# A 528-byte pitch for the blocks of the split activations, in a float32r encoder kernel on Trainium2

## The chip, the cores and the metric

The kernel runs on one core of one Trainium2 chip. The metric is the device time of one execution in microseconds (us), as the median of several runs. TensorE does the products, ScalarE (ACT) and VectorE (DVE) prepare their operands and read their results, GpSimd (POOL) does small work, and SyncE (SP) issues the loads of the weights.

## The reference

A trunk of two layers over 256 tokens of width 1024. Each layer is x += 1/2 SwiGLU(RMSNorm(x)), then a mixer (a gated delta rule in both directions, and a latent attention, merged by gates), then a second SwiGLU. What matters here is the number of dense products:

```python
def swiglu(x, w_gate, w_up, w_down):
    return (jax.nn.silu(x @ w_gate) * (x @ w_up)) @ w_down   # 1024 -> 2816 -> 1024, four times
h = rmsnorm(x, norm_mix[l])
... = split_cols(h @ w_in[l])                                # 1024 -> 4784, twice
x = x + (gates[:, :, 0] * y_a + gates[:, :, 1] * y_b) @ w_out[l]
```

## The kernel before

Every dense product is done in float32r, with each operand split into a high and a low half that are both exact in that type. Three passes make one product: high by high, high by low, low by high. `mm3` (lines 129 to 135) issues them, and its three matmul lines are L133, L134 and L135:

```python
for t in ts:
    a1, a2 = (v[:, t * P:(t + 1) * P] for v in a)
    T.matmul(ps[t][:, :n], lhsT=a1, rhs=w[0], start=start, stop=False)
    T.matmul(ps[t][:, :n], lhsT=a1, rhs=w[1], start=False, stop=False)
    T.matmul(ps[t][:, :n], lhsT=a2, rhs=w[0], start=False, stop=stop)
```

The stationary operand (`lhsT`, loaded into the array by a weight load of its own before each matmul) is a block of activations, 128 channels by 128 tokens, which is 512 bytes in each partition. The moving operand (`rhs`) is a strip of the weight matrix of up to 512 columns, 2048 bytes in each partition. So TensorE reads two places of SBUF in turn for each product: the 512 bytes of the next block, and the 2048 bytes of the running strip.

The activations lie in pairs of tiles. `xh` and `xl` (halves of the normed x, [128, 8 chunks, 256 tokens]) feed the gate and up products and the input projection of the mixer. `hh` and `hl` ([128, 22 chunks, 256 tokens]) feed the down products of SwiGLU. `fr2` tiles ([128, 2 chunks, 256 tokens]) feed the smaller products of the mixer. In all of them a chunk takes 1024 bytes, token tile 0 and token tile 1 of 512 bytes each, with nothing between.

One group of lines has the roles swapped. `qkv_group` (L536) loads a 128 by 128 block of the weights as stationary operand and moves all 256 tokens of a chunk of `xh` or `xl` past it.

The tiles are placed one behind the other in each partition. In the compiled program of this kernel their first bytes are, counted modulo 512: `xh` 0, `xl` 0, the three buffers each of the weight halves `whi` and `wlo` 0, `hh` and `hl` 64, `fr2` 96. For the last down product the kernel takes the weights of the last six chunks from a pool of its own (`fin`, in `finale`); those buffers start at 64 modulo 512. Strips of 512 columns start at 0 or 2048 bytes in their buffer.

The weights come from HBM in transfers of up to 1 MB on SP's queue (`raw`), ACT rounds them to the high half (L122), DVE makes the low half (L123). The activations are turned by transposes on TensorE into PSUM (`to_chan`, L183), and `split` writes the two halves: L104 and L105 for `hh` and `hl`, L107 and L108 with a gain for `xh` and `xl`. Order on each engine is chosen when the program is built, by a planner that simulates a timeline; it keeps the order of the code where priorities say so and fills gaps with what is ready.

Of the kernel before, what the change touches and what calls it, by code (L numbers as in the profile page):

```python
# [11 lines left out]
F32 = mybir.dt.float32  # L12
F32R = mybir.dt.float32r
# [7 lines left out]
P = 128  # L21
D = 1024
# [15 lines left out]
def encoder_trunk(ctx: ExitStack, tc: tile.TileContext, x, positions, norm_ffn1, ffn1_w_gate, ffn1_w_up,  # L38
# [23 lines left out]
    # the tensor engine's clock rises while the first loads run  # L62
# [8 lines left out]
    # columns of gains: ffn1 (8 per layer), mix, ffn2, q latent (3), kv latent (2), gdn (1)  # L71
# [21 lines left out]
    xh = main.tile([P, NKC, S], F32R, name="xh")  # L93
    xl = main.tile([P, NKC, S], F32R, name="xl")
# [6 lines left out]
    def split(hi, lo, ps, gain=None):  # L101
        """hi + lo = gain * ps, both exact in float32r."""
        if gain is None:
            A.copy(out=hi, in_=ps)  # L104
            V.tensor_tensor(out=lo, in0=ps, in1=hi.bitcast(F32), op=ALU.subtract)  # L105
        else:
            A.activation(out=hi, in_=ps, func=AF.Copy, scale=gain)  # L107
            V.scalar_tensor_tensor(out=lo, in0=ps, scalar=gain, in1=hi.bitcast(F32), op0=ALU.mult,  # L108
                                   op1=ALU.subtract)

    def weights(src, nk, w, pool=wpool):
        """A [nk*128, w] slice of weights, as (hi, lo) tiles of up to 1024 elements a partition."""
        raw = wpool.tile([P, 2048], F32, tag="raw", name="raw", bufs=3)
        nc.sync.dma_start(out=raw[:, :nk * w].rearrange("p (k c) -> p k c", c=w),
                          in_=src.rearrange("(k p) c -> p k c", p=P))
        per = 1024 // w
        res = []
        for k0 in range(0, nk, per):
            n = min(per, nk - k0)
            hi = pool.tile([P, 1024], F32R, tag="whi", name="whi", bufs=3)  # L120
            lo = pool.tile([P, 1024], F32R, tag="wlo", name="wlo", bufs=3)
            A.copy(out=hi[:, :n * w], in_=raw[:, k0 * w:(k0 + n) * w])  # L122
            V.tensor_tensor(out=lo[:, :n * w], in0=raw[:, k0 * w:(k0 + n) * w], in1=hi[:, :n * w].bitcast(F32),  # L123
                            op=ALU.subtract)
            for k in range(n):
                res.append((hi[:, k * w:(k + 1) * w], lo[:, k * w:(k + 1) * w]))
        return res

    def mm3(ps, a, w, n, start, stop, ts=range(NT)):
        """ps[t] (+)= a^T w in three passes, for the token tiles ts."""  # L130
        for t in ts:
            a1, a2 = (v[:, t * P:(t + 1) * P] for v in a)
            T.matmul(ps[t][:, :n], lhsT=a1, rhs=w[0], start=start, stop=False)  # L133
            T.matmul(ps[t][:, :n], lhsT=a1, rhs=w[1], start=False, stop=False)  # L134
            T.matmul(ps[t][:, :n], lhsT=a2, rhs=w[0], start=False, stop=stop)  # L135

    def dense_t(acts, src, c0, w, evac, tail=4, pool=wpool):
        """evac(t, psum [128 tokens, w]) of acts @ src[:, c0:c0+w]; acts: (hi, lo) [128, tokens] of each chunk.
        The last chunks (tail or fewer) go through for one token tile, then for the other."""
# [19 lines left out]
    def dense(ah, al, nk, src, c0, w, evac, **kw):  # L159
        dense_t([(ah[:, k, :], al[:, k, :]) for k in range(nk)], src, c0, w, evac, **kw)  # L160

    def dense_halves(acts, parts):
        """dense_t for two parts (src, c0, evac) of 512 columns: the first half of the chunks for both, then the second."""
# [11 lines left out]
    def to_chan(srcs, hi, lo, kc, gain0=None):  # L175
        """Transposes srcs[t] ([128 tokens, n*128]) into chunks kc.. of hi / lo [128, chunk, tokens]."""
        n = srcs[0].shape[1] // P
        for j in range(0, n, 2):
# [6 lines left out]
            if gain0 is None:  # L185
                split(hi[:, kc + j:kc + j + m, :], lo[:, kc + j:kc + j + m, :],
                      pt[:, :m * S].rearrange("p (c s) -> p c s", s=S))
            else:
                for i in range(m):
                    g = gain0 + j + i  # L190
                    split(hi[:, kc + j + i, :], lo[:, kc + j + i, :], pt[:, i * S:(i + 1) * S], gcol[:, g:g + 1])
# [7 lines left out]
    def x_done(t, cg):  # L199
        """Half cg of x's tile t is final: sum of squares."""  # L200
        A.activation(out=junk, in_=x_sb[:, t, cg * 512:(cg + 1) * 512], func=AF.Square,
                     accum_out=state["ss"][:, t, cg:cg + 1])
# [28 lines left out]
    def ffn(w_gate, w_up, w_down, next_gain, hook=None):  # L231
# [3 lines left out]
        with tc.tile_pool(name="ffn", bufs=1) as fp:  # L235
            hh = fp.tile([P, NFC, S], F32R, name="hh")
            hl = fp.tile([P, NFC, S], F32R, name="hl")
            for c0 in range(0, DFF, 512):
# [17 lines left out]
                else:  # L256
                    dense_halves([(xh[:, k, :], xl[:, k, :]) for k in range(NKC)],
# [12 lines left out]
    def finale(down):  # L270
        """The last x, its norm, the result; x of the first half lies by its gains before the second is there."""
# [37 lines left out]
    def mixer_consts(tmp):  # L309
# [16 lines left out]
        alog = const.tile([P, depth, 8], F32, name="alog")  # -exp(A_log)  # L326
# [12 lines left out]
        # m[p, f]  # L339
# [6 lines left out]
        # half[:, 0]: partition % 32 < 16, half[:, 1]: the others  # L346
# [7 lines left out]
        # the off-diagonal 16-blocks of the 32-blocks on the diagonal: below it (mlo) and above it (mup)  # L354
# [11 lines left out]
        # rotary tables  # L366
# [42 lines left out]
    def mixer(l, next_gain):  # L409
# [7 lines left out]
        with tc.tile_pool(name="mix", bufs=1) as mp:  # L417
# [16 lines left out]
            def rstd_row():  # L434
                """rstd along the free axis, the same in every partition."""
# [26 lines left out]
            def to_chan2(srcs, gains):  # L462
                """Chunks of 128 channels, two to a tile: a list of (hi, lo) [128, tokens]."""
                n = srcs[0].shape[1] // P
                res = []
                for j in range(0, n, 2):
# [13 lines left out]
                    res += [(hi[:, i, :], lo[:, i, :]) for i in range(m)]  # L480
# [18 lines left out]
            def gdn_scalars():  # L499
# [4 lines left out]
                # softplus(a) = max(a, 0) + log1p(exp(-|a|))  # L504
# [14 lines left out]
            qkT = mp.tile([P, 8, S], F32, name="qkT")  # L519
            vT = {}  # lies in ysb until ysb is written  # L520
# [4 lines left out]
            def qkv_group(grp):  # L525
                """Two of the twelve chunks of channels."""
# [3 lines left out]
                # one group of sums after the other: they share a bank. The second takes the weights from the last on  # L530
                for c in range(2):
                    cc = slice(c * P, (c + 1) * P)
                    terms = [m for kc, (wh, wlo) in enumerate(ws)
                             for m in ((wh, xh[:, kc, :]), (wh, xl[:, kc, :]), (wlo, xh[:, kc, :]))]
                    for i, (w, a) in enumerate(terms[::-1] if c else terms):
                        T.matmul(pc[:, c], lhsT=w[:, cc], rhs=a, start=(i == 0), stop=(i == len(terms) - 1))  # L536
# [16 lines left out]
                # 2 silu(.); the lengths and |k| v below take account of the 2  # L553
# [5 lines left out]
            def lengths(c0):  # L559
                """1/|.| of four of the eight heads of q and k, a column for each head."""  # L560
                pss = gdp()[:, :4 * NT * 32].rearrange("p (c t s) -> p c t s", c=4, t=NT)
                for c in (0, 2):
# [3 lines left out]
                    for g in range(4):  # L566
                        # the sums for the tokens of group g, in each of its partitions
# [28 lines left out]
            def mla_dense(hf):  # L596
                """q, k, v of four heads, token-major, rotary parts turned."""
# [22 lines left out]
            def mla_heads(q, k, v):  # L620
                """attend(pair of heads), of the four that q, k, v hold."""
# [15 lines left out]
                def attend(c):  # L637
# [36 lines left out]
                    oT.append((hi[:, c, :], lo[:, c, :]))  # L674
# [4 lines left out]
            LA, Z, egc, cs = {}, {}, {}, {}  # L679
            LAd = {}  # L680
            for d in range(2):
                LAd[d] = mp.tile([P, NT, NH, 2, P], F32, name=f"LA{d}")  # [.., 0, :] for q, [.., 1, :] for k
# [7 lines left out]
            def gdn_coeffs():  # L690
# [3 lines left out]
                # -beta / |k|^2  # L694
# [17 lines left out]
            def gdn_decay(t):  # L712
                """E[j, h, i]: decay from token j to token i of the tile, 0 where i comes before j."""
                for d in range(2):
# [10 lines left out]
                    if t == d:  # L725
                        # first tile of this direction: decay of each token up to the carried state
# [5 lines left out]
                    # hi_m[p, f] holds where f is at or after p in this direction  # L732
# [25 lines left out]
            def gdn_base():  # L758
                """XC, ZC: inverses (and transposes) of the 16-blocks on the diagonal, each block in a partition of its
                own meanwhile."""  # L760
# [47 lines left out]
            def inv_zero():  # L808
                """Z = X^T = (1 + L)^-T from the inverted 16-blocks: blocks of 32, 64, 128 in turn."""
# [23 lines left out]
            def inv2(d):  # L833
# [9 lines left out]
                # the 64-block that the last step takes X from  # L843
# [41 lines left out]
            def gdn_first(d):  # L885
                """First tile of direction d: its solution, and what it adds to the other tile."""
# [39 lines left out]
            def gdn_out(t):  # L926
# [10 lines left out]
                # o here is -|q| sqrt(128) times the true one, zs_t is 2 silu(z) / rstd  # L937
# [118 lines left out]
    new_norm()  # L1056
    state["squares"] = False  # of the input: once its products run
# [32 lines left out]
```

## Time and profile before

| what | value |
|---|---|
| median of 3 runs | 1267.02 us (1266.68 to 1269.48) |
| span of the profiled execution, first to last instruction | 1260.2 us |
| median less span | 6.8 us |
| TensorE busy | 98% of the span |
| mean granted TensorE clock | 0.993 |

The device time of the profiled execution itself isn't recorded beside its span; the median of the runs lies 6.8 us above the span, and that is taken as what lies around it. In the rows below PE is TensorE's matmul side and PEld its weight loads. Each matmul's duration in the rows overlaps with the next one's, so the time that a product costs is the distance from one start to the next, and not the duration.

### The profile page before, as it was taken

Reading aid. Unit: us, or ns where it says so; the run is one execution under the profiler, and the core shown is the slowest. Engines: PE = TensorE matmul, PEld = TensorE weight load, DVE = VectorE, ACT = ScalarE, POOL = GpSimd, SP = SyncE. Lnnn points to the kernel's source line nnn. Section 1 sums busy time; section 2 is a strip of 40 time slices with the busy share of each in tenths; the row PEclk is TensorE's granted clock in tenths of the full one; section 3 lists DMA queues with packets and bytes.
Section 4 is the critical chain, followed back from the end, with each engine's and each line's share of the span. In section 5 each row is a group of like instructions: output and inputs, shape, how many; then the busy total and the mean of one; then the engine's idle time right before and its main releaser. Section 6 shows DMA issues by size and latency. Waiting matters only on the chain.

```text
span 1260.2 us, 17612 instructions
## 1 busy us (share of the span) xinstructions
PE 1230.4 (98%) x7064; PEld 1031.9 (82%) x7064; DVE 774.1 (61%) x1127; ACT 623.4 (49%) x911; POOL 132.5 (11%) x237
## 2 busy tenths in 40 slices
PE   9999999899999999999999999998999999999997
PEld 6888889777988788888888888897778787888886
DVE  5655556986757665554555554588876576555554
ACT  6554445546445455443445443465555455544443
POOL 1000001445001000000000000015540000000010
PEclk9999999999999999999999999999999999999999
DMA  7554554435222555555555555543442245565552
GB/s 266 175 197 153 198 184 157 153 119 167 71 99 95 164 176 181 187 169 198 182 187 182 185 167 201 177 147 123 150 162 74 68 134 184 168 199 179 188 184 84
DMA packets 114576, 202.70 MB, mean 161 GB/s; under 512 B 4107, under 2 KB 30399, under 8 KB 114495
## 3 DMA queue, kind: packets, MB, share of 16 engines
q1 hardware_dynamic: 114031, 200.52, 47.8%
q8 instruction: 55, 0.90, 0.3%
q10 hardware_dynamic: 464, 1.06, 0.2%
q14 instruction: 26, 0.21, 0.1%
HBM read 200.52 MB, written 1.05 MB: 160 GB/s over the span
## 4 chain that ended last, share of the span: by engine, by line
PE 88%; DVE 4%; POOL 4%; issue 1%; ACT 1%; DMA 0%; POOLq 0%; SPq 0%; ACTq 0%
PE acc L133 24%; PE acc L134 23%; PE acc L135 23%; PE acc L536 4%; PE ms L183 2%; DVE wlo L123 2%; POOL bt L783 1%; PE ms L671 1%; PE ms L642 1%; POOL t L785 1%; PE gd L134 1%; PE gd L135 1%; PE gd L133 1%; PE gd L912 1%; DVE cv L551 1%
## 5 line engine op out<-in xcount | busy, mean ns | idle before, releaser
L123 DVE TENSOR_TENSOR wlo<-raw,whi 128x1024 fp32r<-128x1024 f32 (+3 forms) x388 | 471.2, 1217 | 371.0 <-ACT whi L122 369.0
L122 ACT CAST whi<-raw 128x1024 fp32r<-128x1024 f32 (+3 forms) x388 | 398.8, 1031 | 435.9 <-PE acc L135 392.0
L134 PE MATMUL acc<-wlo,xh 128*128 128x512 f32 (+3 forms) x968 | 360.7, 374 | 0.0
L135 PE MATMUL acc<-whi,xl 128*128 128x512 f32 (+3 forms) x968 | 357.5, 372 | 0.0
L133 PE MATMUL acc<-whi,xh 128*128 128x512 f32 (+3 forms) x968 | 344.9, 376 | 0.1
L134 PEld LDWEIGHTS acc<-wlo,xh 128*128 128x128 f32 x968 | 182.4, 188 | 29.8 <-issue 0.4
L133 PEld LDWEIGHTS acc<-whi,xh 128*128 128x128 f32 x968 | 181.4, 188 | 30.4 <-ACT xh L107 0.8
L135 PEld LDWEIGHTS acc<-whi,xl 128*128 128x128 f32 x968 | 182.1, 188 | 29.3
L134 PE MATMUL acc<-wlo,hh 128*128 128x512 f32 x352 | 138.9, 395 | 0.0
L135 PE MATMUL acc<-whi,hl 128*128 128x512 f32 x352 | 138.7, 394 | 0.0
L133 PE MATMUL acc<-whi,hh 128*128 128x512 f32 x352 | 129.1, 397 | 0.0
L135 PEld LDWEIGHTS acc<-whi,hl 128*128 128x128 f32 x352 | 65.9, 187 | 16.1
L133 PEld LDWEIGHTS acc<-whi,hh 128*128 128x128 f32 x352 | 65.9, 187 | 15.9
L134 PEld LDWEIGHTS acc<-wlo,hh 128*128 128x128 f32 x352 | 65.9, 187 | 15.3
L133 PE MATMUL acc<-whi,fr 128*128 128x512 f32 (+1 forms) x152 | 60.9, 407 | 9.2 <-DVE pre L543 7.9
L134 PE MATMUL acc<-wlo,fr 128*128 128x512 f32 (+1 forms) x152 | 61.0, 404 | 0.0
L135 PE MATMUL acc<-whi,fr 128*128 128x512 f32 (+1 forms) x152 | 58.2, 400 | 2.3 <-DVE fr L108 2.3
L536 PE MATMUL acc<-xl,whi 128*128 128x256 f32 x192 | 55.6, 289 | 0.0
L536 PE MATMUL acc<-xh,whi 128*128 128x256 f32 x192 | 55.5, 291 | 0.0
L536 PE MATMUL acc<-xh,wlo 128*128 128x256 f32 x192 | 53.3, 288 | 0.0
L551 DVE SCALAR_TENSOR_TENSOR cv<-pre,ccol,cv 128x256 f32<-128x256 f32 x96 | 51.6, 569 | 0.0
L246 ACT ACTIVATE sil<-acc,rstd 128x512 f32<-128x512 f32 (+1 forms) x48 | 31.0, 654 | 29.5 <-PE acc L135 29.4
(298 smaller groups left out, 1273.3 us busy)
## 6 DMA issues: line engine op xcount, KB each, us to landing
raw<-in_ffn_w_up_dram SPq DMA_DIRECT2D x40, 1024.0 KB, 4.9
raw<-in_ffn_w_down_dram SPq DMA_DIRECT2D x40, 1024.0 KB, 4.9
raw<-in_ffn_w_gate_dram SPq DMA_DIRECT2D x38, 1024.0 KB, 4.9
raw<-in_w_in_dram SPq DMA_DIRECT2D x32, 1024.0 KB, 4.8
raw<-in_w_out_dram SPq DMA_DIRECT2D x8, 1024.0 KB, 4.8
raw<-in_ffn_w_gate_dram SPq DMA_DIRECT2D x12, 512.0 KB, 3.5
raw<-in_ffn_w_up_dram SPq DMA_DIRECT2D x8, 512.0 KB, 3.5
raw<-in_ffn_w_down_dram SPq DMA_DIRECT2D x8, 512.0 KB, 3.3
```

What stands on the lines that cost most here:

```text
L122: A.copy(out=hi[:, :n * w], in_=raw[:, k0 * w:(k0 + n) * w])
L123: V.tensor_tensor(out=lo[:, :n * w], in0=raw[:, k0 * w:(k0 + n) * w], in1=hi[:, :n * w].bitcast(F32), op=ALU.subtract)
L133: T.matmul(ps[t][:, :n], lhsT=a1, rhs=w[0], start=start, stop=False)
L134: T.matmul(ps[t][:, :n], lhsT=a1, rhs=w[1], start=False, stop=False)
L135: T.matmul(ps[t][:, :n], lhsT=a2, rhs=w[0], start=False, stop=stop)
L183: T.transpose(out=pt[:, i * S + t * P:i * S + (t + 1) * P], in_=srcs[t][:, (j + i) * P:(j + i + 1) * P], identity=ident)
L246: A.activation(out=sil[t][:, :w], in_=ps, func=AF.Silu, scale=rstds[0][:, t:t + 1])
L536: T.matmul(pc[:, c], lhsT=w[:, cc], rhs=a, start=(i == 0), stop=(i == len(terms) - 1))
L551: V.scalar_tensor_tensor(out=cv[:, c], in0=pre[:, c, d:d + S], scalar=wc, in1=cv[:, c], op0=ALU.mult, op1=ALU.add)
L642: T.matmul(sc[:, t * S:(t + 1) * S], lhsT=qT[:, t * P:(t + 1) * P], rhs=kT, start=True, stop=True)
L671: T.matmul(po[r:r + MV, :S], lhsT=v[:, kk, h, :], rhs=prT[:, kk, :], start=(kk == 0), stop=(kk == NT - 1))
L783: G.tensor_tensor(out=tv, in0=M[:, b + 1:16, b:b + 1].to_broadcast([P, na, nb]), in1=Y[:, b:b + 1, 0:nb].to_broadcast([P, na, nb]), op=ALU ...
```

## The change

A constant `PITCH = P + 4` is added (132 elements, 528 bytes). `xh`, `xl`, `hh` and `hl` are allocated as [128, chunks, 2, 132] and seen through a view that leaves the last four elements of each row out, so that each 128 by 128 block starts 528 bytes after the one before. Everything that indexes them takes a token tile by its own index. The `fr2` tiles keep their layout and are only viewed in the same form. Comments and docstrings were removed as well.

```diff
+PITCH = P + 4
...
-    xh = main.tile([P, NKC, S], F32R, name="xh")
-    xl = main.tile([P, NKC, S], F32R, name="xl")
+    def pitched(pool, n, name):
+
+        return pool.tile([P, n, NT, PITCH], F32R, name=name)[:, :, :, :P]
+
+    xh = pitched(main, NKC, "xh")
+    xl = pitched(main, NKC, "xl")
...
         for t in ts:
-            a1, a2 = (v[:, t * P:(t + 1) * P] for v in a)
+            a1, a2 = (v[:, t, :] for v in a)
...
-                split(hi[:, kc + j:kc + j + m, :], lo[:, kc + j:kc + j + m, :],
-                      pt[:, :m * S].rearrange("p (c s) -> p c s", s=S))
+                split(hi[:, kc + j:kc + j + m], lo[:, kc + j:kc + j + m],
+                      pt[:, :m * S].rearrange("p (c t s) -> p c t s", t=NT, s=P))
...
-                    split(hi[:, kc + j + i, :], lo[:, kc + j + i, :], pt[:, i * S:(i + 1) * S], gcol[:, g:g + 1])
+                    split(hi[:, kc + j + i], lo[:, kc + j + i],
+                          pt[:, i * S:(i + 1) * S].rearrange("p (t s) -> p t s", s=P), gcol[:, g:g + 1])
...
-            hh = fp.tile([P, NFC, S], F32R, name="hh")
-            hl = fp.tile([P, NFC, S], F32R, name="hl")
+            hh = pitched(fp, NFC, "hh")
+            hl = pitched(fp, NFC, "hl")
...
-                    res += [(hi[:, i, :], lo[:, i, :]) for i in range(m)]
+                    res += [tuple(v[:, i, :].rearrange("p (t s) -> p t s", s=P) for v in (hi, lo)) for i in range(m)]
...
-                        T.matmul(pc[:, c], lhsT=w[:, cc], rhs=a, start=(i == 0), stop=(i == len(terms) - 1))
+                        T.matmul(pc[:, c].rearrange("p (t s) -> p t s", s=P), lhsT=w[:, cc], rhs=a, start=(i == 0),
+                                 stop=(i == len(terms) - 1))
```

## Rows read from the trace of the kernel before

**Rows 1.** The page: busy TensorE, and the lines of the chain that ended last

```profile
PE 1230.4 (98%) x7064; PEld 1031.9 (82%) x7064; DVE 774.1 (61%) x1127; ACT 623.4 (49%) x911; POOL 132.5 (11%) x237
...
PE acc L133 24%; PE acc L134 23%; PE acc L135 23%; PE acc L536 4%; PE ms L183 2%; DVE wlo L123 2%; POOL bt L783 1%; PE ms L671 1%; PE ms L642 1%; POOL t L785 1%; PE gd L134 1%; PE gd L135 1%; PE gd L133 1%; PE gd L912 1%; DVE cv L551 1%
```

**Rows 2.** Stretches: gate and up of a SwiGLU, its down, a piece of the mixer

```profile
core 0: us, PE busy (x) PEld busy (x) DVE busy (x) ACT busy (x) POOL busy (x), PEclk, DMA share, GB/s
444.00:558.00 114.00, 114.00 (x524) 94.24 (x523) 63.32 (x68) 57.14 (x70) 0.70 (x1) 1.00 0.54 175
...
570.00:633.00 63.00, 63.00 (x280) 50.66 (x279) 31.12 (x32) 26.50 (x31) 0.00 (x0) 1.00 0.55 184
...
249.00:256.00 7.00, 6.29 (x27) 5.98 (x27) 3.36 (x5) 3.46 (x7) 1.04 (x1) 0.55 0.21 75
```

**Rows 3.** TensorE's groups by form: count, busy us, mean ns of one

```profile
L133 PE MATMUL acc<-whi,xh 128*128 128x512 f32 x776 | 290.0, 395 | 0.1
...
L133 PE MATMUL acc<-whi,hh 128*128 128x512 f32 x352 | 129.1, 397 | 0.0
...
L536 PE MATMUL acc<-xh,whi 128*128 128x256 f32 x192 | 55.5, 291 | 0.0
...
L133 PE MATMUL acc<-whi,xh 128*128 128x256 f32 x128 | 35.9, 285 | 0.0
L183 PE MATMUL ms<-ident,h 128*128 128x128 f32 x176 | 27.0, 272 | 0.0
L642 PE MATMUL ms<-qk 96*128 96x256 f32 x64 | 17.3, 392 | 0.0
...
L183 PE MATMUL ms<-ident,x_sb 128*128 128x128 f32 x96 | 15.0, 278 | 1.2 <-DMA x_sb<-in_x_dram 1.2
...
L741 PE MATMUL gd<-qkT 128*128 128x256 f32 x32 | 8.4, 385 | 0.4 <-DVE qkT L556 0.4
```

**Rows 4.** Timeline of TensorE, gate and up products of xh: nineteen starts, first and last

```profile
499.70 0.39 PE L133 MATMUL acc<-whi,xh 128*128 128x512 f32 x1
...
503.78 0.39 PE L133 MATMUL acc<-whi,xh 128*128 128x512 f32 x1
```

**Rows 5.** Timeline of TensorE, down products of hh: fourteen starts, first and last

```profile
160.77 0.39 PE L135 MATMUL acc<-whi,hl 128*128 128x512 f32 x1
...
163.80 0.39 PE L133 MATMUL acc<-whi,hh 128*128 128x512 f32 x1
```

**Rows 6.** The same with weights of the finale's own pool: twenty-nine starts

```profile
1245.96 0.39 PE L134 MATMUL acc<-wlo,hh 128*128 128x512 f32 x1
...
1252.31 0.39 PE L135 MATMUL acc<-whi,hl 128*128 128x512 f32 x1
```

**Rows 7.** Timeline of TensorE, products of fr2: eight starts, first, second, third and last

```profile
406.86 0.39 PE L133 MATMUL acc<-whi,fr 128*128 128x512 f32 x1
407.09 0.40 PE L134 MATMUL acc<-wlo,fr 128*128 128x512 f32 x1
407.33 0.40 PE L135 MATMUL acc<-whi,fr 128*128 128x512 f32 x1
...
408.50 0.39 PE L134 MATMUL acc<-wlo,fr 128*128 128x512 f32 x1
```

**Rows 8.** Timeline, products of xh behind six transposes: ten starts, first and last

```profile
638.43 0.82 PE L183 MATMUL ms<-ident,x_sb 128*128 128x128 f32 x6
...
639.32 0.40 PE L135 MATMUL acc<-whi,xl 128*128 128x512 f32 x1
...
641.41 0.39 PE L135 MATMUL acc<-whi,xl 128*128 128x512 f32 x1
```

**Rows 9.** Timeline, moving operand xh or xl of 256 tokens: thirteen starts

```profile
216.53 0.28 PE L536 MATMUL acc<-xl,whi 128*128 128x256 f32 x1
...
217.97 0.28 PE L536 MATMUL acc<-xl,whi 128*128 128x256 f32 x1
```

**Rows 10.** Timeline, products of fr2 of 384 columns: nine starts, first and last

```profile
252.72 0.52 PE L133 MATMUL acc<-whi,fr 128*128 128x384 f32 x1
...
255.28 0.36 PE L135 MATMUL acc<-whi,fr 128*128 128x384 f32 x1
```

**Rows 11.** The split into xh: TensorE's wait for it (page), its durations (its line)

```profile
L133 PEld LDWEIGHTS acc<-whi,xh 128*128 128x128 f32 x968 | 181.4, 188 | 30.4 <-ACT xh L107 0.8
...
L107 ACT ACTIVATE xh<-ms,gcol x48: 454/474/502, 8.3 to 1072.5; 128x256 fp32r<-128x256 f32 x48
```

More of the change, by code (lines that the diff above doesn't have):

```diff
@@ L159, in dense @@
     def dense(ah, al, nk, src, c0, w, evac, **kw):
-        dense_t([(ah[:, k, :], al[:, k, :]) for k in range(nk)], src, c0, w, evac, **kw)
+        dense_t([(ah[:, k], al[:, k]) for k in range(nk)], src, c0, w, evac, **kw)
     def dense_halves(acts, parts):
@@ L256, in ffn @@
                 else:
-                    dense_halves([(xh[:, k, :], xl[:, k, :]) for k in range(NKC)],
+                    dense_halves([(xh[:, k], xl[:, k]) for k in range(NKC)],
                                  [(w_gate, 0, ev_gate), (w_up, 0, ev_up)])
@@ L533, in qkv_group @@
                     terms = [m for kc, (wh, wlo) in enumerate(ws)
-                             for m in ((wh, xh[:, kc, :]), (wh, xl[:, kc, :]), (wlo, xh[:, kc, :]))]
+                             for m in ((wh, xh[:, kc]), (wh, xl[:, kc]), (wlo, xh[:, kc]))]
                     for i, (w, a) in enumerate(terms[::-1] if c else terms):
-                        T.matmul(pc[:, c], lhsT=w[:, cc], rhs=a, start=(i == 0), stop=(i == len(terms) - 1))
+                        T.matmul(pc[:, c].rearrange("p (t s) -> p t s", s=P), lhsT=w[:, cc], rhs=a, start=(i == 0),
+                                 stop=(i == len(terms) - 1))
                 if grp >= 4:
@@ L673, in attend @@
                     split(hi[:, c, :], lo[:, c, :], po[:, :S])
-                    oT.append((hi[:, c, :], lo[:, c, :]))
+                    oT.append(tuple(v[:, c, :].rearrange("p (t s) -> p t s", s=P) for v in (hi, lo)))
                 return attend
```

## The prediction, as it was put on record before the result

> **What bounds the kernel now.** I read the page first. TensorE is busy for 98% of the span, and the chain that ended last runs for 70% through three lines, the three passes of `mm3` [rows 1]. The stretches say the same by stage: in a gate and up stage and in a down stage TensorE is busy for all of the 114 and the 63 us, at granted clock 1.00, with VectorE and ScalarE busy for about half and the DMA engines at 0.55 [rows 2]. So what a change is worth here is how it alters the distance between the starts of two products, times the number of products.
>
> The timeline gives that distance. Products of `xh` and `xl` with 512 columns start 4.08 us / 18 = 226.7 ns apart [rows 4]. Products of `hh` and `hl`, of the same form, start 3.03 / 13 = 233.1 ns apart [rows 5]. Those of `fr2` take 1.64 / 7 = 234.3, in an uneven pattern from 230 to 240 [rows 7]. Durations can't show this, since they overlap (395 and 397 ns) [rows 3].
>
> The products differ in where the stationary block lies. Take the distance, modulo 512 bytes, from the start of the moving strip to the start of the block: 0 for `xh`, 64 for `hh`, 96 for `fr2`. The control is the finale: there `hh` meets weights that also lie at 64, the distance is 0, and the spacing is 6.35 / 28 = 226.8 [rows 6]. The same tile, the same form, 6.3 ns less. So the place of the block against the strip counts, and distance 0 is the cheapest of the three.
>
> A second row says how the 226.7 comes about. Behind six transposes the products of `xh` need nine starts at 2.09 / 9 = 232 ns before they fall into the steady 226.7 [rows 8]. I read the 226.7 as a pace into which equal distances let the array settle, and 232 as what it pays while it hasn't.
>
> In the mixer, while the granted clock is at 0.55 on average, 384 columns take 2.56 / 8 = 320 ns [rows 2, 10]: exactly one column per cycle of the level 1.2 GHz, with nothing on top. By that, 512 columns at 2.4 GHz would be 213.3 ns (an estimate), and the excess of 13 to 21 ns belongs to the full clock, where the strip is consumed twice as fast.
>
> **The change part by part.** *The distances.* `xh` and `xl` start at 0, 33 x 256 = 8448 bytes each, so `xl` now starts at 256 and the weight tiles stay at 0. Block j (two to a chunk) of `xh` is at distance 16 j, 0 to 240; of `xl` at 256 to 496. `hh` starts at 64 as before and `hl` at 256, and their 44 blocks go once round all distances in steps of 16. `fr2` moves by 512 bytes in all and keeps 96. So every product of `xh` and `hh` gets another distance than the one before.
>
> *xh, 512 columns.* 3 x 776 = 2328 products. 176 / 4 + 96 / 4 = 68 interruptions by transposes [rows 3] already cost about seven unsettled starts each, 476 in all; 1852 run at 226.7. With a distance that changes each time I don't expect them to settle. The unseen distances are bounded from below by 213.3, the excess gone, and from above by the largest step in the uneven pattern, 240 [rows 7]. Nearest are the unsettled 232, and the steady 233.1 and 234.3 at other distances; I take 232: 1852 x 5.3 = +9.8 us.
>
> *hh, 512 columns.* 3 x 352 = 1056 products [rows 3], from 233.1 to 232: -1.2 us. The 28 of the finale lose their distance 0: +0.2.
>
> *256 columns.* 3 x 128 with the block stationary and 3 x 192 of L536 with it moving [rows 3], 120 ns each (1.44 / 12) [rows 9], excess 13.3. Bounds: the excess gone, -12.8 us; 240 less 226.7 on each, +12.8. I take 0. Now the moving operand of L536 is two pieces with a gap of 16 bytes. L741 has moved two separate pieces all along, at 385 ns a matmul, against 392 for L642, which moves one [rows 3], so the gap gets no price.
>
> *The splits.* ScalarE and VectorE write rows of 128 with gaps. L107 takes 474 ns, and TensorE waited 0.8 us for it in all [rows 11]; VectorE and ScalarE are free for half of each stage [rows 2], which hides any slowdown. If that cover were gone at the start of a stage, 50 ns on each of the 48 calls would be 2.4 us; I take +0.2. Loads and queues are unchanged.
>
> Sum: 9.8 - 1.2 + 0.2 + 0.2 = +9.0 us. The span goes from 1260.2 to 1269.2; with the 6.8 us between span and median, 1276.0.
>
> The Trainium skill ("TensorE: Matmul & The Clock Gate", Part 2, step 1) says that TensorE has two independent read ports, and that loading the next tile's weights takes no bandwidth from the running matmul. By that the sum would be 0; the finale's row doesn't agree, as 6.3 ns hang on the place alone. The same page (Part 1, on the measured gap) gives about 215.7 ns between 512-column matmuls that follow each other. No steady stretch here is that low, and if the pitch led there, the products of 512 columns would lose 2328 x 11 + 1056 x 17.4 = 44 us and more (an estimate from that page).
>
> **The rivals.** *Faster: the equal pitch is the trouble.* If the excess is a collision of the two reads, the same one for each block because all lie 512 bytes apart, a changing distance takes most collisions away. For it speaks that the whole excess is gone at the lower clock [rows 10], so that it can be avoided in principle. Against it speaks that the two distances other than 0 are dearer, not cheaper [rows 5, 7]. It decides from a point that can be worked out: the present sum over 512 columns is 1852 x 226.7 + 476 x 232 + 1056 x 233.1, which is 229.4 ns on average over 3384. Below an average of 228.7 the kernel is faster by over 0.2%. At half the steady excess, 220 ns, it saves 9.4 x 3384 = 32 us and some 6 on the 256 columns: 1229. At 226.7 for all it saves 9, 1258. I put this rival at about 1245.
>
> *No change.* The new mean over all distances happens to lie within 0.7 ns of 229.4, or the two reads don't meet at all and rows 5 and 6 differ for another cause, such as ScalarE's and VectorE's idleness at the end. Against the second: the gate stage holds 226.7 with both engines as busy as in the down stage [rows 2, 4]. Both give 1267, the first with a chance of 0.10, the second with 0.05. The second is where the two read ports of the Trainium skill ("TensorE: Matmul & The Clock Gate", Part 2) would lead.
>
> *The planner.* Access patterns of another shape can shift its simulated times and so the order in the mixer, where the clock drops [rows 2]. Eighteen products at 320 ns instead of some 174 (384 / 512 of 232) cost 2.6 us. One such spell more or less in each layer is 5 us, on either side; it widens the range and isn't the likeliest by itself.
>
> **How the numbers follow.** Forecast, unsettled pace everywhere, 0.58; no change 0.15; faster 0.27. A difference of 0.2% (2.5 us) is about what a measurement of this kernel can tell. The predicted time is 1276. The forecast's own range is 1270 to 1290 (230 to 236 ns on the steady `xh` products, the 256 columns up to 4 ns worse). The range for 8 in 10 goes down to 1246, which leaves out about half of the faster rival, and up to 1290, which leaves out 0.06.
>
> **What would show it.** Right: in gate and up, starts about 232 ns apart and uneven, with no settling into 226.7; the stretch of 444 to 558 longer by some 2 us; down about the same; L536 near 120; `fr2` as before. Each of these is a step of its own. The steps fail if the gate products stay at 226.7 or go below (then the distance isn't what counts, or small steps of 16 bytes help), if down falls well below 232, or if the 256-column products move. The order of lines on TensorE and the stretches of lower clock tell whether the planner had a part.

## The result, and the profile after

The changed kernel takes 1273.86 us (median of 18 runs, 1267.21 to 1277.18), the kernel before 1266.88 us (18 runs, 1259.20 to 1270.12). The ratio on record is 1.0065, with a 95% interval of 1.0047 to 1.0083 (the quotient of the two medians alone is 1.0055, which lies inside it). The change makes the kernel slower, by 7.0 us between the medians; 1276.0 was forecast. Executions of either kernel spread over some 10 us, at mean granted clocks between 0.985 and 0.995. So beside the medians I use two profiled executions at nearly the same clock: before 1260.2 us of span at 0.993, after 1265.5 us at 0.994. The difference is +5.3 us.

The page after, busy time and the chain that ended last (lines 133 to 135 are now 138 to 140, L536 is L542, L183 is L188):

```profile
span 1265.5 us, 17612 instructions
...
PE 1236.0 (98%) x7064; PEld 1029.5 (81%) x7064; DVE 774.0 (61%) x1127; ACT 623.1 (49%) x911; POOL 132.4 (10%) x237
...
PE acc L138 24%; PE acc L139 23%; PE acc L140 23%; PE acc L542 4%; PE ms L188 2%; DVE wlo L128 2%; POOL t L792 1%; PE ms L678 1%; POOL bt L790 1%; PE ms L649 1%; PE gd L139 1%; PE gd L138 1%; PE gd L140 1%; PE gd L919 1%; DVE cv L558 1%
```

Beside [rows 1], counts are the same, and shares to within 1%. TensorE's matmul side is busy for longer, by 5.6 us; VectorE, ScalarE and GpSimd keep their times to 0.3 us. The compiled programs have the same instructions with the same waits in the same order on every engine. So nothing was added and nothing was reordered. The time must lie in how closely the matmuls follow each other.

The stretches of after that answer to [rows 2], cut at the first starts of the stages (us, busy time of each engine, granted clock, DMA share, GB/s):

```profile
309.50:338.80 29.30, 28.23 (x498) 25.42 (x496) 21.17 (x46) 13.61 (x29) 5.57 (x18) 1.00 0.25 80
443.50:559.60 116.10, 116.10 (x522) 94.18 (x520) 63.15 (x68) 56.90 (x70) 0.69 (x1) 1.00 0.54 172
571.80:634.30 62.50, 62.50 (x278) 50.76 (x277) 31.05 (x32) 26.52 (x31) 0.00 (x0) 1.00 0.54 185
```

Three stretches of before with the same instructions:

```profile
308.60:339.70 31.10, 29.68 (x497) 26.82 (x496) 21.15 (x46) 13.52 (x29) 5.82 (x19) 0.95 0.23 77
444.10:557.90 113.80, 113.80 (x522) 94.12 (x521) 63.15 (x68) 57.04 (x70) 0.70 (x1) 1.00 0.54 176
570.20:633.20 63.00, 63.00 (x279) 50.61 (x278) 31.12 (x32) 26.50 (x31) 0.00 (x0) 1.00 0.55 184
```

Gate and up takes 116.1 us instead of 113.8, with TensorE busy for all of it in both; down takes 0.5 us less. The stretch of the mixer around L542 takes 1.8 us less, and there the granted clock is 1.00 instead of 0.95.

The timeline of TensorE after, in gate and up, against [rows 4]:

```profile
498.96 0.39 PE L140 MATMUL acc<-whi,xl 128*128 128x512 f32 x1
499.19 0.62 PE L138 MATMUL acc<-whi,xh 128*128 128x512 f32 x2
499.65 0.40 PE L139 MATMUL acc<-wlo,xh 128*128 128x512 f32 x1
499.89 0.39 PE L140 MATMUL acc<-whi,xl 128*128 128x512 f32 x1
...
503.38 0.40 PE L138 MATMUL acc<-whi,xh 128*128 128x512 f32 x1
```

Nineteen steps (a row x2 holds two starts) take 4.42 us, 232.6 ns each, where it was 226.7. (Starts are shown to 0.01 us, so a step worked out from two of them, here and below, is good to about 1 ns; the means are from starts in ns.) In down, against [rows 5], fourteen steps take 3.25 us, 232.1 ns each, where it was 233.1:

```profile
579.74 0.40 PE L140 MATMUL acc<-whi,hl 128*128 128x512 f32 x1
...
582.99 0.40 PE L139 MATMUL acc<-wlo,hh 128*128 128x512 f32 x1
```

The products of 256 columns with `xh` or `xl` moving, against [rows 9], take twelve steps in 1.41 us, 117.5 ns each, where it was 120:

```profile
215.82 0.28 PE L542 MATMUL acc<-xl,whi 128*128 128x256 f32 x1
...
217.23 0.28 PE L542 MATMUL acc<-xl,whi 128*128 128x256 f32 x1
```

The mean over all intervals of a kind in the trace, worked out from the starts of consecutive products (pauses over 245 ns left out):

| products | intervals | before, ns | after, ns | sum, us |
|---|---|---|---|---|
| xh, xl, 512 columns | 2245 | 227.6 | 232.4 | +10.7 |
| hh, hl, 512 columns | 1024 | 233.1 | 231.8 | -1.3 |
| fr2, 512 columns | all | 234.0 | 234.0 | 0.0 |
| 256 columns, block stationary | 3 x 128 | 119.9 | 118.1 | -0.6 |

The rest is the mixer's. The L542 stretch of layer 0 is 1.9 us shorter, that of layer 1 0.4 us, and the spell at the lower clock in the products of 384 columns [rows 10] 1.0 us. Of what L542's own products gained, 1.8 us, only some 0.6 us are narrower steps (119.5 ns before, 118.4 after, pauses left out). The rest is the clock: in before, 14 of their steps, at 327 to 330 us, took 213 or 214 ns at a granted clock of 0.50, that is at 1.2 GHz, and in after none did. All of it adds up to some +5.5 us, against +5.3 by the spans.

### The profile page after: what moved, and what is told of

Read it like the earlier page. It is cut to its first block, busy times and chain, and to the rows that moved or that the text cites. A ratio compares the mean times of both kernels' runs of the same rounds, so it can differ in the third digit from the quotient of the medians.

```text
span 1265.5 us, 17612 instructions
## 1 busy us (share of the span) xinstructions
PE 1236.0 (98%) x7064; PEld 1029.5 (81%) x7064; DVE 774.0 (61%) x1127; ACT 623.1 (49%) x911; POOL 132.4 (10%) x237
## 4 chain that ended last, share of the span: by engine, by line
PE 88%; DVE 5%; POOL 4%; issue 1%; ACT 1%; DMA 0%; POOLq 0%; SPq 0%; ACTq 0%
PE acc L138 24%; PE acc L139 23%; PE acc L140 23%; PE acc L542 4%; PE ms L188 2%; DVE wlo L128 2%; POOL t L792 1%; PE ms L678 1%; POOL bt L790 1%; PE ms L649 1%; PE gd L139 1%; PE gd L138 1%; PE gd L140 1%; PE gd L919 1%; DVE cv L558 1%
## 5 line engine op out<-in xcount | busy, mean ns | idle before, releaser
L542 PE MATMUL acc<-xh,whi 128*128 128x256 f32 x192 | 54.7, 286 | 0.0
L542 PE MATMUL acc<-xl,whi 128*128 128x256 f32 x192 | 54.6, 284 | 0.0
L542 PE MATMUL acc<-xh,wlo 128*128 128x256 f32 x192 | 52.4, 283 | 0.0
```

The source lines that it names most:

```text
L542: T.matmul(pc[:, c].rearrange("p (t s) -> p t s", s=P), lhsT=w[:, cc], rhs=a, start=(i == 0), stop=(i == len(terms) - 1))
```

## The experiments

"Distance" is the one of the prediction: from the start of the moving strip to the start of the stationary block. The runs of before beside them had medians of 1264.17 (first four), 1264.24 (next four) and 1259.41 us (one run, last two).

**1. Every block at distance 0, equal pitch.** `hh` and `hl` move into one tile with a lead, and a longer `pre` moves `fr2`; `xh` is at 0 already.

```diff
-            hh = fp.tile([P, NFC, S], F32R, name="hh")
-            hl = fp.tile([P, NFC, S], F32R, name="hl")
+            ht = fp.tile([P, 2 * NFC * S + 112], F32R, name="ht")
+            hh, hl = (ht[:, o:o + NFC * S].rearrange("p (k s) -> p k s", s=S) for o in (112, NFC * S + 112))
...
-                pre = t2("pre", 1, (P, 2, S + 4))
+                pre = t2("pre", 1, (P, 2 * (S + 4) + 104))[:, :2 * (S + 4)].rearrange("p (c s) -> p c s", c=2)
```

> The kernel before with its 512-byte pitch, and hh, hl (64 before) and fr2 (96 before) moved so that their blocks too start at the same place modulo 512 as the strips of the weights; order of instructions as before. Theory (the distance between block and strip sets the pace, and 0 lets the products settle at 226.7 ns): hh goes from 233.1 to 226.7 ns, fr2 from 234.3 to 226.7, xh stays at 226.7; 1056 x 6.4 + 384 x 7.6 = 9.7 us less at most, about 8 us less with unsettled starts behind interruptions, ratio about 0.994. Rival (rows 5 and 6 differ because the engines are idle in the finale): hh stays at 233, ratio 1.000.

Measured: 1256.54 us, ratio 0.9943 (0.9924 to 0.9961), faster than both kernels. Timeline, products of `hh` (now `ht`) and of `fr2`:

```profile
589.62 0.39 PE L135 MATMUL acc<-whi,ht 128*128 128x512 f32 x1
...
590.52 0.62 PE L133 MATMUL acc<-whi,ht 128*128 128x512 f32 x2
...
593.01 0.39 PE L135 MATMUL acc<-whi,ht 128*128 128x512 f32 x1
```

```profile
405.65 0.39 PE L135 MATMUL acc<-whi,fr 128*128 128x512 f32 x1
...
408.83 0.39 PE L135 MATMUL acc<-whi,fr 128*128 128x512 f32 x1
```

Fifteen steps of `hh` take 3.39 us, 226.0 each [rows 5: 233.1]; fourteen of `fr2` 3.18, 227.1 [rows 7: 234.3]. The means are 227.1 and 227.6, so some 1028 x 6.0 + 384 x 6.4 = 8.6 us less, against 7.6 by the medians. Place alone sets 6 ns a product, and the rival of idle engines in the finale is out. The Trainium skill ("TensorE: Matmul & The Clock Gate", Part 2) says that the load of the next weights takes no read bandwidth from the running matmul. That would not lead one to expect these 6 ns; whether they come from the load, no run shows.

**2. Equal pitch, other distances: x at 16, hh at 32, fr2 at 256.**

```diff
-    xh = main.tile([P, NKC, S], F32R, name="xh")
-    xl = main.tile([P, NKC, S], F32R, name="xl")
+    xt = main.tile([P, 2 * NKC * S + 128], F32R, name="xt")
+    xh, xl = (xt[:, o:o + NKC * S].rearrange("p (k s) -> p k s", s=S) for o in (4, NKC * S + 4))
```

(`hh` and `hl` as in experiment 1, with a lead of 120 elements; `pre` 40 elements longer.)

> The kernel before with its 512-byte pitch, where all blocks of a tile keep one equal distance to the strips, but not 0: 16 bytes for xh and xl, 32 for hh and hl, 256 for fr2 (480 for hh in the finale). Settling theory (equal distances let the products settle, whatever the distance; only a changing one can't): each tile shows one fixed or short repeating pattern, and xh lies below 230 ns; the time is within 5 us of before. Rival A (only distance 0 is cheap): xh 232 to 234 all the time, hh 233, fr2 234; 1852 x 6 = 11 us slower, ratio 1.009. Rival B (blocks that start off a 64-byte edge are dear): xh at 16 and hh at 32 at 232 or more, fr2 at 256 near 226.7.

Measured: 1270.66 us, ratio 1.0062 (1.0038 to 1.0085). Two stretches of gate and up:

```profile
459.69 0.39 PE L133 MATMUL acc<-whi,xt 128*128 128x512 f32 x1
...
463.99 0.39 PE L134 MATMUL acc<-wlo,xt 128*128 128x512 f32 x1
```

```profile
482.81 0.39 PE L135 MATMUL acc<-whi,xt 128*128 128x512 f32 x1
483.04 0.63 PE L133 MATMUL acc<-whi,xt 128*128 128x512 f32 x2
...
485.84 0.63 PE L133 MATMUL acc<-whi,xt 128*128 128x512 f32 x2
...
486.77 0.40 PE L133 MATMUL acc<-whi,xt 128*128 128x512 f32 x1
```

Distance 16 runs in either of two ways: nineteen steps in 4.30 us (226.3), or seventeen in 3.96 (232.9), the latter a run of six spacings that repeats. Its mean is 231.1. At 32, `hh` alternates between some 232 and 235 (mean 233.3); at 256, `fr2` falls to a steady 226.7 (mean 228.0). So 0 isn't the only cheap distance, and an equal distance isn't enough to make a product cheap.

**3. The pitch on x only**, and **4. on hh only.** Each puts the other pair back, from after:

```diff
-            hh = pitched(fp, NFC, "hh")
-            hl = pitched(fp, NFC, "hl")
+            hh, hl = (fp.tile([P, NFC, NT, P], F32R, name=n) for n in ("hh", "hl"))
```

```diff
-    xh = pitched(main, NKC, "xh")
-    xl = pitched(main, NKC, "xl")
+    xh, xl = (main.tile([P, NKC, NT, P], F32R, name=n) for n in ("xh", "xl"))
```

> The change for xh and xl alone; hh and hl keep the 512-byte pitch and the distance 64. Theory: xh at 232 ns as in the changed kernel, hh steady at 233.1; the whole loss and a little more, 8 to 9 us slower than before, ratio 1.007. Rival (the loss comes from hh, or from the two together): ratio near 1.000.

> The change for hh and hl alone; xh and xl keep the 512-byte pitch and the distance 0. Theory: xh settles at 226.7 as before, hh goes from 233.1 to about 232; 1 to 1.5 us faster than before, ratio 0.999, which a measurement can hardly tell from no change. Rival (a changing distance costs in hh what it costs in xh): 5 us slower, ratio 1.004.

Measured: x only 1274.36 us, ratio 1.0097 (1.0067 to 1.0127), with `xh` at 232.3 and `hh` at 233.1 ns; `hh` only 1267.86 us, ratio 1.0016 (0.9996 to 1.0035), with `xh` at 227.6 and `hh` at 231.8. The whole loss is that of x. What `hh` gives back, 1.3 us by its steps, is less than these medians can tell; it is also covered by the clock here, as 59 steps of the products with x moving took 213 or 214 ns in the profiled execution of this run, against 14 in before.

**5. Equal pitch: x at 128, hh at 192, fr2 at 384**, and **6. x at 384, hh at 448, fr2 at 480.** Experiment 5 is edited so (as in experiment 1, with a lead of 32 elements for `hh` and 72 more for `pre`); experiment 6 has 32 in place of 96 there, a lead of 96 for `hh` and 96 more for `pre`. `xh` itself stays at 0: the longer tile pushes the weight buffers behind it to 384 modulo 512 in experiment 5 and to 128 in experiment 6, which makes the distance of x 128 and 384.

```diff
-    xh = main.tile([P, NKC, S], F32R, name="xh")
-    xl = main.tile([P, NKC, S], F32R, name="xl")
+    xt = main.tile([P, 2 * NKC * S + 96], F32R, name="xt")
+    xh, xl = (xt[:, o:o + NKC * S].rearrange("p (k s) -> p k s", s=S) for o in (0, NKC * S + 0))
```

> Equal distances again, pitch 512: 128 bytes for xh and xl, 192 for hh and hl (128 in the finale), 384 for fr2. Theory, as the run with 16, 32 and 256 left it: equal distances end in a short repeating pattern, of 226.7 ns on average (0, 256, and part of the stretches at 16) or of about 233.3 (32, 64 and the rest at 16). By multiples of 128 bytes being cheap: xh 226.7, fr2 226.7, hh 233. Rival (only 0 and 256 are cheap): all three at about 233.

> Equal distances, pitch 512: 384 bytes for xh and xl, 448 for hh and hl (384 in the finale), 480 for fr2. Theory (multiples of 128 are cheap): xh 226.7 with 2328 products, hh and fr2 about 233, so the time is that of before within 3 us. Rival (only 0 and 256): xh about 233, 11 us slower. Neither expects a steady pace below 226.7.

Measured, one run each: 1269.66 and 1270.21 us. Timelines of experiment 5, x and then `hh`:

```profile
480.82 0.39 PE L134 MATMUL acc<-wlo,xt 128*128 128x512 f32 x1
...
484.07 0.62 PE L133 MATMUL acc<-whi,xt 128*128 128x512 f32 x2
...
484.76 0.40 PE L135 MATMUL acc<-whi,xt 128*128 128x512 f32 x1
```

```profile
593.80 0.39 PE L135 MATMUL acc<-whi,ht 128*128 128x512 f32 x1
594.03 0.62 PE L133 MATMUL acc<-whi,ht 128*128 128x512 f32 x2
...
596.77 0.39 PE L133 MATMUL acc<-whi,ht 128*128 128x512 f32 x1
```

And experiment 6, x:

```profile
480.66 0.39 PE L135 MATMUL acc<-whi,xt 128*128 128x512 f32 x1
...
484.37 0.63 PE L133 MATMUL acc<-whi,xt 128*128 128x512 f32 x2
484.83 0.40 PE L134 MATMUL acc<-wlo,xt 128*128 128x512 f32 x1
```

Seventeen steps at 128 take 3.94 us (231.8), eighteen at 384 take 4.17 (231.7); the means are 232.4 in both, with the same pattern of seven spacings. At 192 thirteen steps take 2.97 us (228.5), mean 229.2 in a pattern of 226, 229, 232; at 448 mean and pattern are the same. With 0 and 256 that makes three pairs 256 bytes apart that agree. I had forecast 128 as cheap and 192 as dear; both were wrong. `fr2` takes 232.4 at 384, as x does, and 233.3 at 480.

These runs also show that the distance counts and not the block's own place. `xh` lies at 0 as in before, and its step went from 226.7 to 232.4 because the strips moved. And the same `hh` tile that takes 229.0 beside the usual buffers takes 232.4 in the finale of experiment 5, where the weights of the `fin` pool make the distance 128 (35 steps from the first to the last):

```profile
1252.57 0.39 PE L133 MATMUL acc<-whi,ht 128*128 128x512 f32 x1
...
1260.71 0.40 PE L135 MATMUL acc<-whi,ht 128*128 128x512 f32 x1
```

**7. Unequal pitch that keeps to 0 and 256.** Rows of `hh` and `hl` 768 bytes apart; `xl` 256 bytes further, `xh` at 0, so that the distance alternates in both.

```diff
-    xh = pitched(main, NKC, "xh")
-    xl = pitched(main, NKC, "xl")
+    xt = main.tile([P, 2 * NKC * S + 128], F32R, name="xt")
+    xh, xl = (xt[:, o:o + NKC * S].rearrange("p (k t s) -> p k t s", t=NT, s=P) for o in (0, NKC * S + 64))
...
-            hh = pitched(fp, NFC, "hh")
-            hl = pitched(fp, NFC, "hl")
+            ht = fp.tile([P, 2 * NFC * NT * 192 + 128], F32R, name="ht")
+            hh, hl = (ht[:, o:o + NFC * NT * 192].rearrange("p (k t s) -> p k t s", t=NT, s=192)[:, :, :, :P]
+                      for o in (112, NFC * NT * 192 + 112))
```

> Two distances, 0 and 256, in alternation: pitch 512 for xh and xl, with all of xh at 0 and all of xl at 256, so that the distance changes at every third product and back; for hh and hl a pitch of 768, so that it changes from block to block, at every third product at most. Both distances gave 226.7 ns where they were equal throughout. Theory A (each distance has its price): xh about 226.7 to 228 and hh 226.7, some 7 us faster than before. Theory B (what costs is that the distance changes): xh and hh irregular or in another pattern, about 230 to 232; 6 to 11 us slower in xh, 1 to 3 us won in hh.

Measured: 1260.86 us, ratio 0.9959 (0.9935 to 0.9982). Timelines, x and `hh`:

```profile
480.67 0.39 PE L139 MATMUL acc<-wlo,xt 128*128 128x512 f32 x1
...
481.81 0.61 PE L138 MATMUL acc<-whi,xt 128*128 128x512 f32 x2
...
483.85 0.39 PE L138 MATMUL acc<-whi,xt 128*128 128x512 f32 x1
```

```profile
591.70 0.39 PE L139 MATMUL acc<-wlo,ht 128*128 128x512 f32 x1
...
592.83 0.62 PE L138 MATMUL acc<-whi,ht 128*128 128x512 f32 x2
...
594.87 0.39 PE L138 MATMUL acc<-whi,ht 128*128 128x512 f32 x1
```

Fourteen steps take 3.18 and 3.17 us, 227.1 and 226.4 each. A distance that changes with every block costs nothing as long as it stays the same modulo 256. So what makes the change dear isn't that the pitch is other than 512, but that 528 moves the block modulo 256.

**8. Pitch 576 on hh**, the edit of experiment 7 with rows of 144 elements and x at an equal 0: the distance changes in steps of 64 instead of 16.

```diff
-            ht = fp.tile([P, 2 * NFC * NT * 192 + 128], F32R, name="ht")
-            hh, hl = (ht[:, o:o + NFC * NT * 192].rearrange("p (k t s) -> p k t s", t=NT, s=192)[:, :, :, :P]
-                      for o in (112, NFC * NT * 192 + 112))
+            ht = fp.tile([P, 2 * NFC * NT * 144 + 128], F32R, name="ht")
+            hh, hl = (ht[:, o:o + NFC * NT * 144].rearrange("p (k t s) -> p k t s", t=NT, s=144)[:, :, :, :P]
+                      for o in (112, NFC * NT * 144 + 112))
```

> xh and xl as before (pitch 512, distance 0). hh and hl at a pitch of 576 bytes, so that each block starts at a multiple of 64 bytes, at a distance that goes in steps of 64 from block to block. Theory (changing distances keep the products unsettled): hh irregular, 231 to 232 ns on average, as with 528. Rival (528 costs because most blocks start off a 64-byte edge): hh clearly lower than with 528, near 227 to 229.

Measured, one run: 1260.78 us. Timeline of `hh`:

```profile
591.83 0.40 PE L140 MATMUL acc<-whi,ht 128*128 128x512 f32 x1
...
592.76 0.63 PE L138 MATMUL acc<-whi,ht 128*128 128x512 f32 x2
...
595.31 0.39 PE L140 MATMUL acc<-whi,ht 128*128 128x512 f32 x1
```

Fifteen steps take 3.48 us, 232.0 each, mean 231.8, as with 528 and as uneven. That blocks would begin off a 64-byte edge is not the trouble.

**9. Distances that alternate between 0 and 128**: the edit of experiment 7 with `xl` 128 bytes further (`NKC * S + 32`) and rows of 160 elements.

```diff
-    xh, xl = (xt[:, o:o + NKC * S].rearrange("p (k t s) -> p k t s", t=NT, s=P) for o in (0, NKC * S + 64))
+    xh, xl = (xt[:, o:o + NKC * S].rearrange("p (k t s) -> p k t s", t=NT, s=P) for o in (0, NKC * S + 32))
```

> Two distances in alternation that have different settled paces: 0 (226.7 ns) and 128 (232.4 ns). Pitch 512 for xh and xl, all of xh at 0 and all of xl at 128; for hh and hl a pitch of 640, so that the distance changes between 0 and 128 from block to block. Theory P (each distance keeps its own price): xh and xl (2 x 226.7 + 232.4) / 3 = 228.6 ns on average, hh 229.5, and the products at distance 0 stay near 226.7. Theory S (the sequence of distances decides, and a product at 0 between others isn't cheap): a pattern of its own, 231 to 232 in both.

Measured, one run: 1274.01 us. Timeline of x:

```profile
480.76 0.39 PE L138 MATMUL acc<-whi,xt 128*128 128x512 f32 x1
...
483.54 0.62 PE L138 MATMUL acc<-whi,xt 128*128 128x512 f32 x2
...
484.46 0.40 PE L139 MATMUL acc<-wlo,xt 128*128 128x512 f32 x1
```

Sixteen steps take 3.70 us, 231.3 each; the mean is 231.4 for x and 232.5 for `hh`. Theory S had the means right, but not that nothing cheap is left. Once x has settled, its spacings repeat by threes: 226 or 227 ns between two products at distance 0, 232 or 233 from one at 0 to the one at 128, 234 from there back to 0 (means over the trace 228.0, 232.4 and 233.6). `hh` repeats by twelves. So each product at 0 has a cheap step on one side and a dear one on the other. A product isn't cheap by its own place; the places of its neighbours count too.

**10. Shorter loads.** From experiment 1, passes 2 and 3 load only the first 64 tokens, which leaves out the low halves' part for the other 64; in the last chunk the full pass comes last. The order of work shifted a little with it.

```diff
-            T.matmul(ps[t][:, :n], lhsT=a1, rhs=w[0], start=start, stop=False)
-            T.matmul(ps[t][:, :n], lhsT=a1, rhs=w[1], start=False, stop=False)
-            T.matmul(ps[t][:, :n], lhsT=a2, rhs=w[0], start=False, stop=stop)
+            passes = [(P, a1, w[0]), (64, a1, w[1]), (64, a2, w[0])]
+            for i, (c, a_, w_) in enumerate(passes[::-1] if stop else passes):
+                T.matmul(ps[t][:c, :n], lhsT=a_[:, :c], rhs=w_, start=start and i == 0, stop=stop and i == 2)
```

> All tiles at distance 0, as in the fastest kernel so far, and the second and third pass are done for tokens 0 to 63 of each tile alone: their weight loads bring 64 columns in place of 128, while the strips that are moved stay as long (the low halves are left out for the other 64 tokens; in the last chunk the full pass comes last). Theory (the excess over 213.3 ns comes from the next block's load being read beside the running strip): where the next load is of 64 columns the spacing falls by about half of the excess, to some 220 ns, and where it is of 128 it stays near 226.7 or at least higher. Rival (a fixed cost for every change of the stationary block): 226.7 in all places.

Measured, one run: 1269.07 us. Weight loads of both kinds, and the timeline of x:

```profile
L135 PEld LDWEIGHTS acc<-whi,xh 128*128 128x128 f32 x968 | 181.0, 188 | 64.9 <-ACT whi L122 0.5 <-issue 0.4
L135 PEld LDWEIGHTS acc<-wlo,xh 128*64 128x64 f32 x968 | 130.3, 135 | 43.8 <-DVE wlo L123 3.8 <-issue 0.6
```

```profile
480.80 0.39 PE L135 MATMUL acc<-wlo,xh 128*64 128x512 f32 x1
...
481.95 0.61 PE L135 MATMUL acc<-whi,xl 128*64 128x512 f32 x2
...
482.63 0.62 PE L135 MATMUL acc<-whi,xh 128*128 128x512 f32 x2
...
483.77 0.40 PE L135 MATMUL acc<-wlo,xh 128*64 128x512 f32 x1
```

The loads are shorter, 135 instead of 188 ns, but thirteen steps take 2.97 us, 228.5 each. The mean is some 229.5 ns before a short load and before a long one alike. An excess that goes with the length of the load would have given 220 before a short one, a fixed one 226.7; neither number came. Blocks of two lengths in turn are themselves an unequal sequence, so this run can't tell whether the load takes part in the excess. It isn't the same for all forms, either: the products of 256 columns with the block stationary went from 119.7 ns (experiment 1) down to 116.4.

## Why the prediction was right, step by step

- **What bounds it: right.** The loss lies in TensorE's steps, in stretches where it has no idle time.
- **xh at 512 columns: right, in size too.** Forecast 232 ns without settling, +9.8 us; measured 232.4, +10.7. Experiment 3 shows that this is the whole loss.
- **hh and fr2: right.** Forecast -1.2 us and 0; measured -1.3 and 0.0.
- **Why the changing distance costs: partly right.** That the place counts is shown by experiment 1, that a changing place costs by 3 and 9. It isn't so, though, that every product gets another distance than the one before: the first two passes of a block load the same place, and `xl`'s block lies 256 bytes on from `xh`'s modulo 512. So the three passes share one place modulo 256, and a step between two equal places costs no less in the changed kernel (232.3 ns, 1259 steps) than one between different places (232.4, 983). That the changing distance costs the same 232 as the starts behind transposes [rows 8] is an agreement of two numbers; no run shows that they have one cause. But the distance counts modulo 256, not 512 (5, 6, 7), and "equal distances let the array settle" holds only in that the spacings fall into runs that repeat (seen at 16, 32, 128, 192, 384 and 448). Such a run is cheap at 0 and 256 (226.7), less so at 192 and 448 (229.2), and no cheaper than a changing distance at 32 and 128 (233.3, 232.4); at 16 a cheap and a dear one occur. The steps to products at distance 0 modulo 256 in the changed kernel average 232.0, as the others do.
- **256 columns: mis-sized.** The term was 0, within 12.8 us on either side. Those with the block stationary gained 0.6 us by narrower steps, and those of L542 some 0.6 us. That they moved at all was the prediction's own sign that this step had failed. The equal distance of before was not their best place: with x at an equal 16 (experiment 2) L536 takes 117.4 ns a step, against 119.5 at 0. Why is not shown.
- **The splits, the gap of 16 bytes and the planner: right.** VectorE and ScalarE keep their times, and the order is the same.
- **The clock in the mixer: not in the sum.** The changed kernel's profiled execution had shorter spells at the lower clock, some 1 us in [rows 10] and 1.3 us in L542's products. With the 256 columns this is most of the way from the forecast +9.0 to the span's +5.3; such spells come and go over the runs (59 steps of this kind in experiment 4, none in experiment 8), so nothing shows that the change brought it.
- **The 6.8 us from span to median: held, for another reason than was given.** The profiled execution of after took 1267.21 us, 1.7 us more than its span. The rest of the 8.4 us from its span to the median of 1273.86 goes with the clock: 14 of the 18 executions ran at a mean of 0.986 to 0.990, the profiled one at 0.994. That the median came within 2.1 us of the forecast is in part luck: the span was forecast 3.7 us too long and the distance to the median 1.6 us too short.
- **The faster rival** needed a mean below 228.7 over the products of 512 columns. It is 232.2 (2245 at 232.4, 1024 at 231.8). Still, the sign of its idea was right in one place: a better placement than before's exists, and it is one of equal distances (experiment 1).

What stays open is the mechanism. That the time hangs on place and order, the period and the patterns are shown; that the moving read and the weight load get in each other's way was argued from [rows 10] and is not shown by any run. Experiment 10, meant to show it, didn't.

## What to carry to other kernels

Where float32r products of 512 columns, each with a load of its own, follow each other with no pause on TensorE, put all stationary blocks and moving strips at the same place modulo 256 bytes: here that cost a few hundred bytes of a tile and brought 0.6% (experiment 1). Other types and forms were not tried, and products of 256 columns went the other way. Don't pad a pitch by other than a multiple of 256 on a suspicion of collisions; a padding that moves each block modulo 256 cost 5 ns on each of 2328 products that had lain at distance 0. Look for such effects in the distance between starts, as durations overlap and barely move (395 before [rows 3], 399 after).

## What was not expected of the hardware

- The price of a place repeats every 256 bytes: 232.4 ns at 128 and at 384, 229.2 at 192 and at 448, 226.7 at 0 and at 256.
- Spacings of equal products repeat in runs of two (distance 32), three (192), six (16) or seven (128), and one placement (16) can hold either of two runs, 226.7 or some 233.
- The sequence of places sets the step: with two products at 0 and one at 128 in turn, the step between the two at 0 stays at 227 ns, and the steps to and from 128 take 233 and 234.
- Products of 256 columns are cheaper off distance 0: 117.4 to 119.2 ns there (16, 128, 384 and the pitch of 528), and 119.4 to 119.9 on it.
